# A list scheduler's model of the chip, rewritten: costs, PSUM hand-overs, TensorE bursts and the landing of first loads

## The chip, the core and the metric

The kernel runs on one core of a Trainium2 chip. Its engines take instructions from queues of their own, each strictly in order: TensorE (PE, matmuls, with its weight loads, PEld), ScalarE (ACT), VectorE (DVE), GpSimd (POOL) and SyncE (SP, which here only issues DMAs). Matmul results go to PSUM, which has eight banks; data otherwise lies in SBUF and comes from HBM by DMA. The metric is the device time of one execution in microseconds (us), lower is better. Runs of this kernel agree closely: 615.1 to 615.19 us.

## The reference, cut to what matters

Two layers over 256 tokens of width 1024, in float32. Each has a mixing sublayer with three groups of heads (neighbourhood "a", 4 heads; dilated "d", 6; grouped-query "c", 6 on 2 key/value heads) and a gated feed-forward network with a centred convolution of width 3 over the tokens.

```python
def mixer_sublayer(x, n1, w_in_l, qg, kg, rpb_l, og, w_out_l, tables):
    h = rms_norm(x, n1)
    proj = h @ w_in_l                       # 1024 x 2560
    qa, ka, va, qd, kd, vd, qc, kc, vc = jnp.split(proj, cuts, axis=-1)
...
    out_a = neighbourhood_attention(qa, ka, heads(va, H_NA), rpb_l, na_idx, na_dr, na_dc)
...
    out_d = dilated_window_attention(qd, kd, heads(vd, H_DIL), dil_idx, dil_val)
...
    out_c = gqa_block_attention(qc, kc, heads(vc, H_GKV))
    mix = jnp.concatenate([rms_norm(out_a, og[:NA_W]), rms_norm(out_d, og[NA_W:NA_W + DIL_W]),
                           rms_norm(out_c, og[NA_W + DIL_W:])], axis=-1)
    return x + mix @ w_out_l

def channel_sublayer(x, n2, w_gu, cw, cb, w_dn):
    h = rms_norm(x, n2)
    g, u = jnp.split(h @ w_gu, 2, axis=-1)  # 1024 x 5632
    g = depthwise_conv_centred(g, cw, cb)
    return x + (jax.nn.gelu(g, approximate=False) * u) @ w_dn   # 2816 x 1024

for l in range(DEPTH):
    x = mixer_sublayer(...)
    x = channel_sublayer(...)
```

## The kernel before

**Arithmetic.** Every matmul operand is split in two fp32r parts, hi and lo, and a product is made of three matmuls (`mm3`, L636: hi·hi, hi·lo, lo·hi). The weights stream from HBM in units of up to 128 x 2048 floats (`load`, tile `wp_raw`, four buffers); for each unit ACT copies the hi part (`wp_hi`) and DVE subtracts for the lo part (`wp_lo`), two buffers each (`split`, L607), in chunks of 384, 512 or 1024 columns. Activations are split in the same way: the transposed norm hT (`act_hT`), the transposed probabilities (tiles pTch and pTcl, in the trace `act_ch` and `act_cl`), the mixed heads mixT (`act_mixT_hi`, `act_mixT_lo`).

**Stages.** In each layer: the norm's transposes (pt_n1); the projections into PSUM tiles named after their group and half of the tokens (pj_dq, pj_dk, pj_dv, pj_cq, pj_ckv, pj_aqk, pj_av); per group the q and k norms and rotary positions (tiles z, then their transposes tr_q*, tr_k*); the heads in pairs; the output projections po0 to po2 added to the residual xs (in the trace `const_x`) with a group's factor (gs transposes, DVE sum, POOL rstd); then the second norm (pt_n2, h2) and eleven steps of gate G, up U and down D. One head is a chain through four engines: scores (PE), mask and maximum (DVE), two exponentials (ACT), reciprocal (DVE), scaling (ACT), four transposes tp (PE), hi copy pTch (ACT), lo copy pTcl (DVE), the weighted sum o of twelve matmuls for two heads (PE), mixT hi (ACT) and lo (DVE). The scores of two heads are one burst of twelve matmuls with 64-row operands, which use the two halves of the array side by side; the planner keeps them together (`together`). The matmuls of the projections and of po fill the time in which PE would wait for such a chain. Before the first real data PE runs 28 warming matmuls on a tile of ones: 13 with normal rank, 15 (WARM_MORE) with a rank 1000 later, to be used as fill. The neighbourhood bias is built through HBM: POOL repeats it, SP stores it (`scr`) and two loads read it back shifted (`nab`), and DVE masks it in three operations.

**Order.** Nothing above is issued directly: each call is recorded as an operation of class Plan (`add`, L253) with the engine, the operations before it, a rank (its place in the program plus an offset from `later`) and a cost in ns from `cost` (L416). `order` (L303) then simulates the engines. Over all engines' ready operations it takes again and again the one with the smallest (start time, rank); `at_of` (L318) gives the start as the latest of the operation's inputs, its engine's free time and the time at which a buffer or PSUM slot of its pool comes free; `at_of_burst` (L331) does so for a burst. The table HANDOVER (L215) adds the delay from one engine's end to another's start. A DMA is put down with its issue time, a wire shared by its ring and a latency. The result fixes the order of every engine's queue, SP's and POOL's DMAs too; `emit` (L408) issues it, so all instructions of the trace carry line L413. PSUM is two pools of four banks: psa (projections and outputs, `psa_a`) and psw (transposes, scores, o, G and U, `psw_w`). The order matters on the chip alone: which data an operation waits for is kept by semaphores whatever the planner believes.

## Time and profile before

| what | value |
|---|---|
| median of 3 runs | 615.19 us (615.1 to 615.19) |
| the profiled execution, its own time | 615.77 us |
| its span, first to last instruction | 614.0 us |
| mean granted TensorE clock | 0.999 |
| bytes over DMA | 121.44 MB, 198 GB/s |

The profile shows one execution. Its tables give the busy time of each engine, the same by stretches of time, the chain of work that ended last (followed back from the last instruction), and each instruction with its start, duration, engine and output<-input by tile names; `[0.42 <-ACT wp_hi L413]` at a row's end says that the engine was idle for 0.42 us before it and what ended that. Equal neighbours are put into one row with a count (x4), whose duration runs from the first start to the last end. PE's matmuls overlap, so the distance from start to start and not the duration is what one costs; idle time before a row is counted from the modelled end of the one before.

### The profile page before, as it was taken

Reading aid. Unit: us, or ns where it says so; the run is one execution under the profiler, and the core shown is the slowest. Engines: PE = TensorE matmul, PEld = TensorE weight load, DVE = VectorE, ACT = ScalarE, POOL = GpSimd, SP = SyncE. Lnnn points to the kernel's source line nnn. Section 1 sums busy time; section 2 is a strip of 40 time slices with the busy share of each in tenths; the row PEclk is TensorE's granted clock in tenths of the full one; section 3 lists DMA queues with packets and bytes.
Section 4 is the critical chain, followed back from the end, with each engine's and each line's share of the span. In section 5 each row is a group of like instructions: output and inputs, shape, how many; then the busy total and the mean of one; then the engine's idle time right before and its main releaser. Section 6 shows DMA issues by size and latency. Waiting matters only on the chain.

```text
span 614.0 us, 9882 instructions
## 1 busy us (share of the span) xinstructions
PE 604.2 (98%) x3484; PEld 525.1 (86%) x3484; DVE 488.2 (80%) x1000; ACT 428.2 (70%) x1064; POOL 83.4 (14%) x136
## 2 busy tenths in 40 slices
PE   8999999999999999999999999999999999999997
PEld 6998878888888888888899988887888888888885
DVE  4898989898778988877767797867977777787774
ACT  6788989686657676666588898866765556566561
POOL 2732231216000000000023212432000000000000
PEclk9999999999999999999999999999999999999999
DMA  8894212654698999988444744553655556556501
GB/s 281 269 288 161 95 44 79 226 188 164 209 239 293 330 335 320 310 276 284 153 151 155 242 137 173 197 183 112 231 202 176 175 202 191 171 187 206 188 18 68
DMA packets 85073, 121.44 MB, mean 198 GB/s; under 512 B 9864, under 2 KB 69608, under 8 KB 85024
## 3 DMA queue, kind: packets, MB, share of 16 engines
q1 hardware_dynamic: 82752, 112.17, 55.8%
q0 software_dynamic: 1728, 8.39, 4.0%
q8 instruction: 27, 0.44, 0.3%
q10 hardware_dynamic: 544, 0.26, 0.1%
q14 instruction: 22, 0.18, 0.1%
HBM read 110.93 MB, written 9.88 MB: 197 GB/s over the span
## 4 chain that ended last, share of the span: by engine, by line
PE 93%; ACT 2%; DVE 2%; issue 1%; DMA 1%; SPq 1%; POOL 0%; DVEq 0%; ACTq 0%
PE psw_w L413 50%; PE psa_a L413 43%; DVE const_x L413 1%; ACT act_s2k L413 1%; DMA const_x<-in_x_dram 1%; SPq L413 1%; ACT act_hT L413 1%; DVE act_hT L413 0%; ACT wp_hi L413 0%; DVE wp_lo L413 0%; POOL small_rstd L413 0%; ACT act_mixT_hi L413 0%; POOL small_ms L413 0%; DVE act_mixT_lo L413 0%; DVE small_ss L413 0%
## 5 line engine op out<-in xcount | busy, mean ns | idle before, releaser
L413 DVE TENSOR_TENSOR wp_lo<-wp_raw,wp_hi 128x512 fp32r<-128x512 f32 (+2 forms) x332 | 232.5, 733 | 58.4 <-ACT wp_hi L413 33.7
L413 ACT CAST wp_hi<-wp_raw 128x512 fp32r<-128x512 f32 (+2 forms) x332 | 202.3, 662 | 18.9 <-PE psw_w L413 9.6
L413 PE MATMUL psw_w<-act_hT,wp_hi 128*128 128x512 f32 x704 | 180.6, 394 | 0.4 <-DVE act_hT L413 0.4
L413 PEld LDWEIGHTS psw_w<-act_hT,wp_hi 128*128 128x128 f32 x704 | 127.9, 189 | 25.5 <-DVE act_hT L413 1.2
L413 PE MATMUL psa_a<-wp_hi,act_hT 128*128 128x384 f32 (+2 forms) x448 | 112.8, 333 | 1.4 <-ACT act_hT L413 1.3
L413 PEld LDWEIGHTS psw_w<-act_hT,wp_lo 128*128 128x128 f32 x704 | 97.7, 190 | 6.9
L413 PE MATMUL psw_w<-act_hT,wp_lo 128*128 128x256 f32 x704 | 102.5, 283 | 0.0
L413 PEld LDWEIGHTS psa_a<-wp_hi,act_hT 128*128 128x128 f32 x448 | 77.9, 189 | 4.6 <-ACT act_hT L413 1.8
L413 ACT COPY act_s2k<-psw_w 128x256 f32<-128x256 f32 x88 | 32.3, 371 | 63.8 <-PE psw_w L413 63.3
L413 PE MATMUL psa_a<-wp_lo,act_hT 128*128 128x384 f32 (+2 forms) x224 | 74.8, 334 | 0.0
L413 PE MATMUL psa_a<-wp_hi,act_ch 128*128 128x512 f32 x176 | 69.5, 395 | 0.0
L413 PE MATMUL psa_a<-wp_lo,act_ch 128*128 128x512 f32 x176 | 69.4, 395 | 0.0
L413 PE MATMUL psa_a<-wp_hi,act_cl 128*128 128x512 f32 x176 | 68.2, 395 | 0.0
L413 DVE TENSOR_TENSOR act_s2k<-psw_w,act_s2k 128x256 f32<-128x256 f32 x88 | 36.8, 421 | 12.9 <-ACT act_s2k L413 12.6
L413 PEld LDWEIGHTS psa_a<-wp_lo,act_hT 128*128 128x128 f32 x224 | 42.3, 189 | 1.9 <-DVE wp_lo L413 1.0
L413 PEld LDWEIGHTS psa_a<-wp_hi,act_cl 128*128 128x128 f32 x176 | 33.2, 188 | 7.7
L413 PEld LDWEIGHTS psa_a<-wp_hi,act_ch 128*128 128x128 f32 x176 | 33.2, 189 | 6.8
L413 PEld LDWEIGHTS psa_a<-wp_lo,act_ch 128*128 128x128 f32 x176 | 33.2, 189 | 6.8
L413 DVE SCALAR_TENSOR_TENSOR act_s2k<-act_s2k,act_cw,act_s2k 128x255 f32<-128x255 f32 x88 | 37.0, 480 | 1.4 <-ACT act_s2k L413 1.3
L413 ACT ACTIVATE act_s2k<-act_s2k,act_cw 128x256 f32<-128x256 f32 x44 | 24.1, 595 | 17.3 <-DVE act_s2k L413 17.0
L413 ACT ACTIVATE act_s2k<-act_s2k 128x512 f32<-128x512 f32 x22 | 13.9, 631 | 27.9 <-DVE act_s2k L413 27.9
L413 POOL TENSOR_TENSOR small_rstd<-small_ms,const_mh 128x6 f32<-128x6 f32 (+2 forms) x26 | 31.4, 1206 | 2.2
(112 smaller groups left out, 796.0 us busy)
## 6 DMA issues: line engine op xcount, KB each, us to landing
wp_raw<-in_w_gate_up_dram SPq DMA_DIRECT2D x44, 1024.0 KB, 5.2
wp_raw<-in_w_down_dram SPq DMA_DIRECT2D x22, 1024.0 KB, 4.9
wp_raw<-in_w_in_dram SPq DMA_DIRECT2D x14, 768.0 KB, 5.0
wp_raw<-in_w_in_dram SPq DMA_DIRECT2D x8, 1024.0 KB, 5.2
wp_raw<-in_w_out_dram SPq DMA_DIRECT2D x8, 768.0 KB, 4.9
dram_khi<-act_mixT_hi SPq DMA_DIRECT2D x4, 768.0 KB, 4.7
dram_klo<-act_mixT_lo SPq DMA_DIRECT2D x4, 768.0 KB, 5.7
wp_lo<-dram_klo POOLq DMA_DIRECT2D x4, 768.0 KB, 4.8
```

What stands on the lines that cost most here:

```text
L413: getattr(o.engine.real, o.method)(*map(real, o.args), **{k: real(v) for k, v in o.kw.items()})
```

## The change

Only the planner changes. The diff, cut to its core:

```diff
 ]
+LANDS = (4300, 3900, 5250, 3500, 6500, 7080, 7800, 8330, 8900, 9700, 10400, 10500, 10600)
+
+
 WARM, WARM_MORE, WARM_W = 13, 15, 256
 SUM_ACT, SCALE_ACT = ("dq", "dk", "cq"), ("dk",)
...
 HANDOVER = {
-    ("PE", "DVE"): 196, ("PE", "ACT"): 197, ("PE", "POOL"): 224, ("ACT", "DVE"): 131, ("ACT", "POOL"): 61,
-    ("ACT", "PE"): 240, ("DVE", "ACT"): 160, ("DVE", "PE"): 215, ("DVE", "DVE"): 127, ("DVE", "POOL"): 155, ("POOL", "DVE"): 60,
-    ("POOL", "ACT"): 60, ("POOL", "PE"): 150,
+    ("PE", "DVE"): 39, ("PE", "ACT"): 37, ("ACT", "DVE"): 33, ("DVE", "ACT"): 35, ("POOL", "DVE"): 34, ("POOL", "ACT"): 34,
+    ("DVE", "POOL"): 95, ("ACT", "POOL"): 90, ("POOL", "POOL"): 20, ("DVE", "DVE"): 34, ("ACT", "ACT"): 34,
 }
+
+
+def handover(a, b):
+    return HANDOVER.get((a, b), 52 if b == "PE" else 60)
 class Plan:
...
         ins = [v for v in views if not any(v is w for w in outs)]
         if method == "matmul" and not kw["start"]:
             ins.append(args[0])
-        o.ns, o.size = cost(engine.name, method, args, kw, ins)
+        o.ns, o.lat, o.size, o.kind = cost(engine.name, method, args, kw, ins)
         o.before, o.after, o.first, o.tiles = set(), [], [], []
         for v in ins + outs:
             t = v.tile
...
             for t in o.first:
                 t.turn = turns.get(t.pool, 0)
                 turns[t.pool] = t.turn + 1
-                t.left = t.users
-        free = dict.fromkeys(("PE", "ACT", "DVE", "POOL", "SP"), 550.0)
+                t.left, t.last = t.users, {}
+        free = dict.fromkeys(("ACT", "DVE", "POOL", "SP"), 550.0)
+        pe = None
         wires = {}
-        ready = {e: [] for e in free}
+        ready = {e: [] for e in ("PE", *free)}
         for i, o in enumerate(ops):
             o.at = 0.0
             if not o.left:
                 ready[o.engine.name].append(i)
+
+        def idle_at(e):
+            if e != "PE":
+                return free[e]
+            return 550.0 if pe is None else pe[0] + 3
+
+        def taken_at(since, e):
+            return since + (52 if e == "PE" else 36) if since > 0 else 0.0
+
         def at_of(o):
-            at = max(o.at, free[o.engine.name])
+            e = o.engine.name
+            at = max(o.at, idle_at(e))
             for t in o.tiles:
                 s = t.pool
                 if t.slot is not None:
                     at = max(at, t.since)
+                    if s.psum:
+                        for f, end in t.last.items():
+                            if f != e:
+                                at = max(at, end + handover(f, e))
                     continue
                 if t.turn != s.given or not s.free:
                     return None
-                at = max(at, min(s.free)[0])
+                at = max(at, taken_at(min(s.free)[0], e))
             return at
         def at_of_burst(burst):
-            at, wanted = 0.0, {}
+            at, wanted = idle_at("PE"), {}
             members = set(self.bursts[burst])
             for i in self.bursts[burst]:
                 o = ops[i]
                 if any(j not in members and not gone[j] for j in o.before):
                     return None
-                at = max(at, o.at, free[o.engine.name])
+                at = max(at, o.at)
                 for t in o.tiles:
                     if t.slot is not None:
                         at = max(at, t.since)
...
             for s, tiles in wanted.items():
                 if {t.turn for t in tiles} != set(range(s.given, s.given + len(tiles))) or len(s.free) < len(tiles):
                     return None
-                at = max(at, sorted(s.free)[len(tiles) - 1][0])
+                at = max(at, taken_at(sorted(s.free)[len(tiles) - 1][0], "PE"))
             return at
+
+        def run_on_pe(o, at):
+
+            half = o.kind == "half"
+            if pe is None:
+                return at + 109, o.ns, half, False
+            start, ns, was, open_ = pe
+            if half and was:
+                ld = max(start + 3, at)
+                if open_:
+                    return max(start + 4, ld + (0 if at <= start + 3 else 109)), o.ns, half, False
+                return max(start + 113, ld + 109), o.ns, half, True
+            if half or was:
+                return max(start + ns + 92, at) + 108, o.ns, half, True
+            return max(start + ns, max(start + 3, at) + (106 if o.kind == "turn" else 110)), o.ns, half, False
         done = []
         gone = [False] * len(ops)
...
                     s.given += 1
                     place = min(s.free)
                     s.free.remove(place)
-                    t.since, t.slot = place
-            free[e] = end = at + o.ns
+                    t.since, t.slot = taken_at(place[0], ""), place[1]
+            if e == "PE":
+                pe = run_on_pe(o, at)
+                end = pe[0] + o.ns + (218 if o.kind == "turn" else 163)
+            else:
+                free[e], end = at + o.ns, at + o.lat
             if o.method == "dma_start":
                 ring = e if i < self.first_loads else "SP"
-                end = max(end + 900, wires.get(ring, 0.0))
+                end = max(at + 1360, wires.get(ring, 0.0))
                 shared = 0.0
                 if i < self.first_loads:
                     shared = o.size if ring == "ACT" else min(o.size, 120 * max(0.0, wires.get("ACT", 0.0) - end))
                 wires[ring] = end + shared / 120 + (o.size - shared) / (280 if i < self.first_loads else 360)
                 end = wires[ring] + 900
+                if i < self.first_loads:
+                    end = LANDS[sum(p.method == "dma_start" for p in ops[:i])]
             for t in o.tiles:
                 t.left -= 1
                 t.until = max(t.until, end)
+                t.last[e] = end
                 if not t.left:
-                    t.pool.free.append((t.until + 170, t.slot))
+                    t.pool.free.append((t.until, t.slot))
             for j in o.after:
                 a = ops[j]
-                a.at = max(a.at, end + (170 if o.method == "dma_start" else HANDOVER.get((e, a.engine.name), 0)))
+                f = a.engine.name
+                if e != "PE" or f != "PE":
+                    a.at = max(a.at, end + (100 if o.method == "dma_start" else handover(e, f)))
                 a.left -= 1
                 if not a.left:
-                    ready[a.engine.name].append(j)
+                    ready[f].append(j)
         return done
     def emit(self):
...
     if method == "dma_start":
         w = out if isinstance(out, View) else args[1]
         small = min(out.shape[-1], args[1].shape[-1]) < 128
-        return 460, 4 * math.prod(w.shape) * (2 if small else 1)
+        spread = isinstance(args[1], bass.AP) and args[1].ap[0][0] == 0
+        size = 4 * math.prod(w.shape) * (2 if small else 2 if spread else 1)
+        return 620 if engine == "POOL" else 480, 0, size, None
     n = out.width()
     psum = any(v.tile.pool.psum for v in ins)
     if engine == "PE":
         if method == "transpose":
-            return 110, 0
+            return n / 2.25 + 2.5, 0, 0, "turn"
         n = args[2].width()
-        if args[1].dtype == F32:
-            return 108, 0
-        if args[1].shape[0] < P:
-            return n / 4.8 + 15, 0
-        return n / (2.4 if args[1].dtype == F32R else 1.2) + 2.5, 0
+        ns = {512: 231.6, 384: 174.5, 256: 118.0}.get(n, n / 2.25 + 2.5)
+        return ns, 0, 0, "half" if args[1].shape[0] < P else "full"
     if engine == "ACT":
-        extra = 93 * sum(isinstance(kw.get(k), View) for k in ("scale", "bias")) + 90 * ("accum_out" in kw)
-        return 0.833 * n + (47 if psum else 94) + extra, 0
+        extra = 88 * sum(isinstance(kw.get(k), View) for k in ("scale", "bias")) + 92 * ("accum_out" in kw)
+        ns = 0.833 * n + (53 if psum else 95) + extra
+        return ns, ns + (15 if "accum_out" in kw else 105), 0, None
     if engine == "DVE":
         if method in ("reduce_sum", "reduce_max"):
             n = args[1].width()
-        per = 1.04
-        if method in ("tensor_copy", "tensor_scalar_mul") and not psum:
-            per = 0.52
-        if method == "tensor_tensor_reduce":
-            per = 1.3
-        return per * n + (130 if method == "scalar_tensor_tensor" or method == "tensor_scalar_mul" and n > 16 else 70), 0
+        ns = 1.04 * n + (126 if method == "scalar_tensor_tensor" else 68)
+        return ns, ns + 82, 0, None
     if method == "memset":
-        return 40 + 0.9 * n, 0
-    if method == "tensor_copy":
-        return 3.4 * n, 0
-    if kw.get("op") == ALU.pow:
-        return 300 + 165 * n, 0
-    return 2.2 * n + 160, 0
+        ns = 190 + 0.83 * n
+    elif method == "tensor_copy":
+        ns = 0.92 * n + 100
+    elif kw.get("op") == ALU.pow:
+        ns = 560 + 150 * n
+    elif method == "tensor_scalar":
+        ns = 350 + 3.8 * n
+    else:
+        ns = 830 if out.width() == S else 350 + 3.1 * n
+    return ns, ns - 95, 0, None
 @with_exitstack
```

In words. The table HANDOVER becomes small (20 to 95 ns instead of 60 to 240), because `cost` now gives two figures for ACT, DVE and POOL: `ns`, how long the engine is occupied, and `lat`, when the result is there. PE has a model of its own (`run_on_pe`): a matmul starts after its weight load, half-row matmuls (kind "half") run two at a time, and switching between half and full costs extra; operations of PE that depend on PE's own no longer wait in the plan. A tile in PSUM remembers when each engine last used it (`t.last`), and an operation of another engine is put behind that: one engine at a time uses a bank. The DMAs' latency is 1360 ns from issue, POOL's issues cost 620 ns, and the end of each of the 13 first loads comes from the table LANDS. POOL's costs are new too, for example 830 ns for an addition over 256 columns where it was 723.

The programs of both hold the same instructions (3484 matmuls and transposes, the same DMAs); their order on each engine differs.

3 lines of the change are left out of this document (2 added, 1 removed).

## The prediction

> **What bounds the kernel now.** I read the page first: the busy shares, then the chain that ended last.
>
> ```profile
> span 614.0 us, 9882 instructions
> ...
> PE 604.2 (98%) x3484; PEld 525.1 (86%) x3484; DVE 488.2 (80%) x1000; ACT 428.2 (70%) x1064; POOL 83.4 (14%) x136
> ...
> PE 93%; ACT 2%; DVE 2%; issue 1%; DMA 1%; SPq 1%; POOL 0%; DVEq 0%; ACTq 0%
> ```
>
> TensorE (PE) is busy 98% of the span and makes 93% of the chain. The change neither adds nor removes a matmul (3484 in both builds, the DMAs are the same too), so what it can win is PE's idle time and no more. The second view, the busy time by stretches, shows where that is.
>
> ```profile
> core 0: us, PE busy (x) PEld busy (x) DVE busy (x) ACT busy (x) POOL busy (x), PEclk, DMA share, GB/s
> 0.00:14.46 14.46, 12.06 (x70) 9.39 (x70) 5.75 (x15) 8.94 (x23) 3.01 (x12) 1.00 0.86 275
> ...
> 60.00:80.00 20.00, 20.00 (x150) 17.82 (x149) 17.62 (x55) 18.99 (x56) 3.14 (x6) 1.00 0.29 96
> ...
> 82.00:86.00 4.00, 2.51 (x18) 1.94 (x17) 3.37 (x9) 3.08 (x10) 2.62 (x3) 1.00 0.00 0
> 86.00:100.00 14.00, 14.00 (x98) 11.70 (x97) 13.65 (x39) 12.68 (x41) 1.97 (x4) 1.00 0.11 39
> ...
> 120.50:128.00 7.50, 7.02 (x41) 5.58 (x42) 7.36 (x15) 7.19 (x20) 1.72 (x3) 1.00 0.35 136
> 128.00:309.00 181.00, 181.00 (x952) 155.06 (x953) 151.60 (x256) 118.81 (x219) 11.10 (x19) 1.00 0.80 265
> ...
> 382.00:385.00 3.00, 2.44 (x20) 2.24 (x20) 2.85 (x10) 3.00 (x12) 2.81 (x3) 1.00 0.00 0
> ...
> 420.00:426.00 6.00, 5.50 (x31) 4.57 (x32) 4.96 (x11) 5.83 (x15) 0.00 (x0) 1.00 0.02 4
> ```
>
> In the 181 us of the first feed-forward network PE never stops; the second has the same matmuls in the same order. Idle time that an order can touch lies in the attention half of layer 0 (1.49 us between 82 and 86), at the step from attention to the network (0.48 and 0.50), in layer 1's attention (0.56) and at the start (2.40). Of the rest, 60 to 80 says something else: PE at 20.00 of 20, ScalarE (ACT) at 18.99 and VectorE (DVE) at 17.62. What is reordered there has little room on three engines at once.
>
> **The start.** The planner now believes in 109 to 118 ns for a warming matmul and puts all 28 first; before, 15 went first, and the others filled gaps.
>
> ```profile
> 0.98 3.38 PE L413 MATMUL psw_w<-const_warm 128*128 128x256 bf16 x15 [0.98 <-POOL const_warm L413]
> ...
> 4.95 0.60 PE L413 MATMUL psw_w<-const_warm 128*128 128x256 bf16 x4
> ...
> 6.56 0.51 ACT L413 CAST wp_hi<-wp_raw 128x384 fp32r<-128x384 f32 x1 [3.53 <-DMA wp_raw<-in_w_in_dram]
> ...
> 7.49 0.61 PE L413 MATMUL psa_a<-wp_hi,act_hT 128*128 128x384 f32 x2 [1.29 <-ACT act_hT L413]
> ...
> 13.88 2.60 ACT L413 CAST wp_hi<-wp_raw 128x384 fp32r<-128x384 f32 x6
> ...
> 14.46 0.30 PEld L413 LDWEIGHTS psa_a<-wp_hi,act_hT 128*128 128x128 f32 x2 [0.42 <-ACT wp_hi L413]
> ```
>
> Fifteen cold ones took 3.38 us, or 0.21 each after the overlap of the last; warm ones start 0.11 apart (four in 0.60, the last of which fills 0.27 by itself). With the fast state from about 4.9 on, eighteen at 0.21 and ten at 0.11 end near 5.9. Five transposes follow at about 0.11 to 0.2, so the first hT0 on ACT starts near 6.6 and not at 6.97, but ahead of the two hi0 copies, which began at 6.56. The first real matmul therefore comes near 8.0, half a us later than 7.49. That does not move the end: from 6.56 to 16.5 ACT goes almost without a pause, and the matmuls of 14.46 wait for its hi1 copies at 13.88. ACT has the same 16 pieces before hi1 in both orders. I take +0.1, between −0.1 (ACT no longer waits for hT0 in between) and +0.5 (all of the later first matmul).
>
> The granted clock reads 1.00 over this whole stretch, the slow matmuls included, so here only the spacing tells the state: 0.21 up to 4.3, 0.11 from 4.95. The Trainium skill, TensorE: Matmul & The Clock Gate, section What's actually happening, says that the gate opens after about 3.4 us of activity in a free-running window, so that warming buys time and not a count, and that it closes again after an idle window of that length. The trace agrees with the opening; by the rest, the new idle time of about 1.3 us ahead of 8.0, like the 1.29 ahead of 7.49, closes nothing, and the sum stays.
>
> **Attention of layer 0.** The place that loses most is the second pair of the six GQA heads.
>
> ```profile
> 51.17 0.28 PE L413 MATMUL psa_a<-wp_lo,act_hT 128*128 128x256 f32 x1
> ...
> 51.53 0.28 PE L413 MATMUL psa_a<-wp_lo,act_hT 128*128 128x256 f32 x1
> ...
> 80.73 0.98 PE L413 MATMUL psw_w<-act_kc,act_qc 64*128 64x256 f32 x12
> ...
> 82.18 0.47 ACT L413 ACTIVATE const_v<-psa_a,small_rx 128x256 fp32r<-128x256 f32 x1 [0.22 <-PE psa_a L413]
> ...
> 83.00 0.47 ACT L413 ACTIVATE act_s2k<-psw_w,small_nm 128x256 f32<-128x256 f32 x1
> ...
> 83.71 0.36 PE L413 MATMUL psw_w<-act_ch,const_v 128*128 128x256 f32 x1 [1.13 <-ACT act_s2k L413]
> ...
> 85.06 0.46 DVE L413 SCALAR_TENSOR_TENSOR act_mixT_lo<-psw_w,const_gains,act_mixT_hi 128x256 fp32r<-128x256 f32 x1
> ...
> 85.58 0.44 PE L413 MATMUL psw_w<-const_ident,act_z 128*128 128x128 f32 x2 [0.36 <-DVE act_mixT_lo L413]
> ...
> 383.63 0.66 PE L413 MATMUL psw_w<-const_ident,act_s2k 128*128 128x128 f32 x4 [0.56 <-ACT act_s2k L413]
> ...
> 384.05 0.37 PE L413 MATMUL psw_w<-act_ch,const_v 128*128 128x256 f32 x1
> ```
>
> The score burst s_c02/s_c03 ends at 81.7; its bank comes free when ACT's second exponential of head c02 ends at 83.47, and the weighted sum o_06, which takes that bank over, starts at 83.71. So 2.0 us pass from burst to bank. Behind the burst, before has two projection matmuls and four transposes. Three 256-column matmuls take 0.36 (51.17 to 51.53), one 0.12; with transposes at 0.11 (four in 0.42, from 383.63 to 384.05) that is 0.7 us of cover, and 1.3 us of stall. The new order has twenty such matmuls and four transposes there: 2.4 + 0.44 = 2.8 us, more than 2.0. The stall goes: −1.3. It can hold because before spent that fill early: two projection matmuls pj_av were left at the burst, after has 38 left, and the burst stands 36 matmuls earlier on PE. The transposes at 85.58 (waiting for a bank whose last reader is the DVE's 85.06) come behind those twenty too: −0.36.
>
> What is late next? The chain of the heads (scores, maximum, exponential, transposes, hi and lo copies, weighted sum) is asked for up to 36 × 0.12 = 4.3 us earlier against the projections. To serve it, ACT's copies hi11 and hi12 and the V evictions, and DVE's lo10 and lo11, are moved behind it; they feed projections that come later as well, so most of the shift is paid in work that nobody waits for. Two transposes of z_cq01 are an exception: they move ahead of the burst s_d02.
>
> ```profile
> 54.58 0.55 DVE L413 TENSOR_TENSOR act_z<-act_z,act_sw 128x384 f32<-128x384 f32 x1
> ...
> 56.24 0.27 PE L413 MATMUL psw_w<-const_ident,act_z 128*128 128x128 f32 x1
> ```
>
> z is done at 55.13; the new place of the two transposes is five 512-column matmuls earlier, near 55.1. DVE puts z ahead of one lo copy (pTcl_d00) now, so it may come 0.6 earlier and cost nothing, or not, with a wait up to 0.6. I take +0.3. For this stretch −1.3 −0.36 +0.3 = −1.4; bounds −1.7 and 0 (all of it met again in a later wait).
>
> **The mask tables and SP's queue.** The store of the bias rows and the two loads nab0 that read it back go ahead of raw8 and raw9.
>
> ```profile
> L413 DVE SCALAR_TENSOR_TENSOR act_nab<-act_nab,const_na x6: 739/752/761, 44.2 to 203.0; 128x576 f32<-128x576 f32 x6
> ...
> 35.05 1.97 SPq L413 DMA_DIRECT2D act_nab<-dram_scr  x2
> ...
> 39.84 4.36 DVE L413 TENSOR_TENSOR wp_lo<-wp_raw,wp_hi 128x384 fp32r<-128x384 f32 x8
> ...
> 46.71 5.71 PE psa_a L413 x46
> ```
>
> The eight copies from 39.84 on are lo7 and lo8, so lo8 began near 41.7, and nab0 came behind it at 44.2. Now all three nab0 operations (0.75 each) stand in front of lo8. If their data lands no sooner than before, DVE is held 44.2 − 41.7 = 2.5 us and has 3 × 0.75 = 2.25 to do before lo8, whose first copy would end near 47.1 instead of 42.4; the matmuls on it begin with the run of 46.71 or shortly ahead of it, so PE would stand up to 1.0. But the loads now pass raw9 on SP's queue and raw8 comes behind the store, so the data should land sooner, by about the length of a load. I take 0, with 0 and +1.0 as bounds.
>
> **The step to the network, layer 0.**
>
> ```profile
> 119.84 0.40 PE L413 MATMUL psa_a<-wp_hi,act_mixT_lo 128*128 128x512 f32 x1
> ...
> 120.07 0.40 PE L413 MATMUL psa_a<-wp_hi,act_mixT_hi 128*128 128x512 f32 x1
> ...
> 120.59 0.44 PE L413 MATMUL psw_w<-const_ident,const_x 128*128 128x128 f32 x2
> ```
>
> A 512-column matmul takes 0.23 (119.84 to 120.07), so the transposes could have started at 120.30; they waited 0.29 for DVE's residual. The new order sends the norm's transposes gs20 out four matmuls (0.92) sooner, so the residual is ready sooner and the 0.29 goes. DVE and ACT put the copies lo18, lo19, hi18, hi19 behind the h20 chain, for which G0_00 now waits at 127.85: of the 0.48 idle between 120.5 and 128 (0.09 of it belongs to the wait before) I take 0.3. Together −0.6; bounds −0.8 and 0.
>
> **Layer 1** has the same pattern, and the 0.56 ahead of 383.63 is its form of the stall at 83.71.
>
> ```profile
> ...
> 420.12 0.88 PE L413 MATMUL psw_w<-const_ident,const_x 128*128 128x128 f32 x6 [0.48 <-DVE const_x L413]
> ...
> 424.03 0.69 DVE L413 TENSOR_TENSOR wp_lo<-wp_raw,wp_hi 128x512 fp32r<-128x512 f32 x1
> ...
> 425.43 0.88 PE L413 MATMUL psw_w<-const_ident,const_x 128*128 128x128 f32 x6 [0.37 <-DVE const_x L413]
> ```
>
> That stall is covered by the same shift of fill; the transposes of z_cq11 get 0.1 to 0.55 shorter cover, of which I take 0.3: −0.3, bounds −0.6 and +0.2. At the end of its attention the lo69 copy leaves its place (one of 0.69, at 424.03) ahead of the residual and goes into earlier idle time; the 0.37 at 425.43 goes, the 0.48 at 420.12 stays, since the same residual and the same PE order stand before it: −0.4, bounds −0.85 and 0. Stores on SP swap one place with raw loads there, and POOL's loads of stored weights go behind small operations; what they feed is a unit or more away from its use: 0. The feed-forward order is the same: 0.
>
> **Sum:** +0.1 −1.4 +0 −0.6 −0.3 −0.4 = −2.6, and I keep −2.5. The profiled execution took 615.77 us (its span of 614.0 and 1.8 around it), 0.6 over the median of the runs, 615.19; a difference of 2.5 from either gives 612.7 in the runs. Bounds of all terms: −0.1 −1.7 −0.8 −0.6 −0.85 = −4.05, and +0.5 +1.0 +0.2 = +1.7.
>
> **Rivals.**
>
> *The heads' chain is late (slower).* In 86 to 100 DVE has 13.65 of 14 and in 60 to 80 ACT has 18.99 of 20. If DVE can't pull the lo copies pTcl forward, because each meets one weight copy of 0.69 that is already in the queue, PE waits 0.69 once at each of the six pairs of d and c heads in layer 0: +4.1. Against the −2.5 that is +1.6: 616.8. It makes the whole thing slower than the measurable bound from 0.62 a pair on, (2.5 + 1.23)/6. For it: no slack on three engines. Against it: DVE as a whole does no more work, the deferred copies are those, and only one wait of the six was there before.
>
> *The stalls move (same).* What 83.71, 85.58 and 383.63 win is met again in the next waits, since ACT and DVE and not PE then set the pace of the heads; left are the steps to the network, −0.6 −0.4, with +0.1 at the start and +0.3 for z: 614.6. For it: the same rows.
>
> *DVE waits for the masks.* All of the −2.5, with the +1.0 for nab0 and another +0.5 from what DVE then does late: 614.2, within the bound below too.
>
> *The planner is wrong and the change doesn't do what it says.* It counts 118 ns for a cold matmul that took 0.21, and places first loads by a table; all its later times are then off by half a us, and waits between DMA, ACT and PE fall otherwise than planned: no gain, and +0.5 at the start, 615.7.
>
> **How the numbers follow.** I call a difference under 0.2% (1.23 us) the same, which is what a measurement of this kernel can't tell from none. The forecast, 612.7, gets 0.56, its own range being 611.1 to 613.9; the late chain 0.20; moved stalls, masks and a planner gone wrong together 0.24. Some 0.02 of the forecast's chance ends above 613.96: faster 0.54, same 0.26, slower 0.20. The range goes from 610.9, the lower bound with 0.2 for what I haven't seen, to 616.6, about the middle of the late chain.
>
> **What would show it.** Right: PE busy without a pause from 80 to 86, the row of o_06 without an ACT releaser; transposes of const_x without a DVE releaser at 120 and 425; the first pj matmul near 8.0 but hi1's matmuls at 14.4 to 14.6; feed-forward stretches at 181 of 181. Wrong: new waits of 0.3 us or more of PE for pTcl, mixT_lo or act_z between 55 and 100; DVE idle ahead of act_nab on a DMA; matmuls at twice their spacing after 8 us; or a hi1 that comes after 14.9.

## The result, and the profile after

The changed kernel is slower: 620.64 us (617.0 to 623.99, 9 runs) against 615.19 us (614.78 to 615.69, 9 runs) of the kernel before on the same chip, a ratio of 1.0077 (of the means, as all ratios here) with an interval of 1.005 to 1.0105. Its nine runs lie further apart than those of before, and the time goes with the mean granted clock: 617.0 and 617.02 us at 1.000, 618.52 at 0.999, and 619.6 to 623.99 in the six at 0.994 to 0.998. The profiled execution is the one of 623.99, so the 8.2 us between the two spans overstate the 5.45 between the medians.

The page of the changed kernel (span; busy times; shares of the chain that ended last):

```profile
span 622.2 us, 9882 instructions
...
PE 609.7 (98%) x3484; PEld 527.8 (85%) x3484; DVE 484.6 (78%) x1000; ACT 428.3 (69%) x1064; POOL 85.1 (14%) x136
...
PE 87%; DMA 4%; DVE 4%; ACT 2%; issue 1%; POOL 1%; SPq 1%; DVEq 0%; ACTq 0%; POOLq 0%
```

The work is the same. The chain shows what is new: DMA is now 4% of it, where before it was 1%, and PE lost 6 points. PE's busy time grew by 5.5 us for the same 3484 matmuls; the slow clock below is a part of that. Where the span grew, by the start times of the same matmuls in the two traces (from one named matmul to the next):

| stretch | after − before, us |
|---|---|
| start to the first matmul on hi1 | +3.51 |
| to the first down matmul of layer 0 (attention, step, G0_00) | −1.64 |
| to the first projection of layer 1 (the feed-forward network) | +1.90 |
| to the first down matmul of layer 1 | +4.45 |
| the rest | 0.00 |

**Start.** The timeline of the changed kernel, first 18 us:

```profile
0.98 6.02 PE L459 MATMUL psw_w<-const_warm 128*128 128x256 bf16 x28 [0.98 <-POOL const_warm L459]
...
7.46 1.28 ACT L459 ACT_TABLE_LOAD   x1 [7.46 <-DVE const_gains L459]
8.76 0.84 ACT L459 ACTIVATE act_hT<-psw_w,const_gains 128x256 fp32r<-128x256 f32 x2
...
10.05 0.94 PE L459 MATMUL psa_a<-wp_hi,act_hT 128*128 128x384 f32 x2 [2.30 <-ACT wp_hi L459]
...
17.97 0.62 PE L459 MATMUL psa_a<-wp_hi,act_hT 128*128 128x384 f32 x2 [0.38 <-ACT wp_hi L459]
```

Three things are to be seen. The 28 warming matmuls take 6.02 us, 0.21 each to the last. The table load of ACT stands right in front of its first activation, hT0, and waits with it for DVE's `const_gains`, which is read from the first transpose; in before, the same load had this row:

```profile
1.74 1.28 ACT L413 ACT_TABLE_LOAD   x1 [1.74 <-issue]
```

ACT's first piece there was a hi0 copy, which waited for its DMA until 6.56; the load ran ahead of that wait. And PE then has 2.30 us without work. How the clock goes on in this profile is in the view by stretches (length, busy time and count of PE, PEld, DVE, ACT and POOL, then PEclk, DMA share, GB/s):

```profile
8.00:9.00 1.00, 0.00 (x0) 0.00 (x0) 0.00 (x0) 0.99 (x2) 0.00 (x0) 1.00 1.11 314
...
10.00:11.00 1.00, 0.95 (x4) 0.85 (x5) 1.00 (x4) 1.00 (x4) 0.00 (x0) 0.58 1.03 376
...
12.00:13.00 1.00, 1.00 (x5) 1.00 (x4) 0.64 (x3) 1.00 (x3) 0.00 (x0) 0.50 1.02 344
...
13.50:14.00 0.50, 0.50 (x4) 0.50 (x4) 0.23 (x1) 0.24 (x1) 0.00 (x0) 0.93 1.04 372
...
416.00:418.00 2.00, 0.41 (x2) 0.00 (x0) 1.14 (x2) 0.27 (x1) 1.25 (x2) 1.00 0.86 233
...
419.00:420.00 1.00, 1.00 (x5) 0.83 (x4) 0.00 (x0) 0.00 (x0) 0.00 (x0) 0.88 0.85 238
420.00:421.00 1.00, 1.00 (x4) 0.71 (x4) 0.00 (x0) 0.00 (x0) 0.00 (x0) 0.50 0.60 217
...
423.00:424.00 1.00, 1.00 (x5) 0.76 (x5) 0.00 (x0) 0.00 (x0) 0.39 (x1) 0.92 0.00 0
```

Behind the idle gap of 2.30 us the clock is at one half from about 10.2 to 13.6, behind one of 1.82 us ahead of 418.24 from about 419.8 to 423.2. (The edges come from the means: 0.58 in a stretch of 1.00 is 0.84 us at one half, so it fell at 10.16.) PE counts as fully busy there; it is only slower. A gap of this length did not always have this behind it, as p_new_start below shows.

**Feed-forward network, layer 0.** The timeline of the changed kernel at a stored weight, and the same place before:

```profile
214.44 0.37 SPq L459 DMA_DIRECT2D wp_raw<-in_w_out_dram  x1
...
226.34 1.66 ACT L459 CAST act_mixT_hi<-wp_raw 128x512 fp32r<-128x512 f32 x3 [2.62 <-DMA wp_raw<-in_w_out_dram]
...
227.91 0.36 ACT L459 COPY act_s2k<-psw_w 128x256 f32<-128x256 f32 x1
...
228.17 0.62 ACT L459 CAST act_ch<-act_s2k 128x512 fp32r<-128x512 f32 x1
...
228.84 0.50 PE L459 MATMUL psa_a<-wp_hi,act_ch 128*128 128x512 f32 x1 [0.90 <-ACT act_ch L459]
```

```profile
223.58 0.62 ACT L413 CAST act_mixT_hi<-wp_raw 128x512 fp32r<-128x512 f32 x1
...
224.10 0.62 ACT L413 CAST act_ch<-act_s2k 128x512 fp32r<-128x512 f32 x1
...
224.62 0.62 ACT L413 CAST act_mixT_hi<-wp_raw 128x512 fp32r<-128x512 f32 x1
```

While the first network runs, the output weights of layer 1 are split once for later: loaded, copied to hi by ACT and to lo by DVE (in the trace through buffers named `act_mixT_hi` and `act_mixT_lo`), stored by SP, and read back by POOL's loads in layer 1. I call them stored weights. Before, `act_ch`, for which the down matmuls wait, stood between their copies; after, all three stand ahead of it, and wait for a load that took 11.88 us. Counted from start to start of the matmuls, PE loses 1.06 us there and 0.57 at the next lo part.

**Layer 1.** POOL and PE of the changed kernel, then POOL of before:

```profile
409.42 0.57 POOL L459 DMA_DIRECT2D wp_lo<-dram_klo  x1 [2.18 <-PE psa_a L459]
...
410.35 0.71 POOL L459 TENSOR_TENSOR small_rstd<-small_ms,const_mh 128x2 f32<-128x2 f32 x1
...
411.02 0.60 POOL L459 DMA_DIRECT2D wp_hi<-dram_khi  x1
...
418.24 0.50 PE L459 MATMUL psa_a<-wp_hi,act_mixT_hi 128*128 128x512 f32 x1 [1.82 <-DMA wp_hi<-dram_khi]
```

```profile
401.63 0.57 POOL L413 DMA_DIRECT2D wp_lo<-dram_klo  x1 [4.15 <-PE psa_a L413]
402.20 0.54 POOL L413 DMA_DIRECT2D wp_hi<-dram_khi  x1
```

The hi load of the stored weight hi66 goes out 1.60 us after that of lo66 instead of 0.57, behind the small operations `small_ms` and `small_rstd`, and lands at 418.19, when PE has been waiting for it. PE loses 1.98 us from start to start, and the slow clock follows.

### The profile page after: what moved, and what is told of

It is laid out like the page before. It is cut to its first block, busy times and chain, and to the rows that moved or that the text cites. A ratio compares the mean times of both kernels' runs of the same rounds, so it can differ in the third digit from the quotient of the medians.

```text
span 622.2 us, 9882 instructions
## 1 busy us (share of the span) xinstructions
PE 609.7 (98%) x3484; PEld 527.8 (85%) x3484; DVE 484.6 (78%) x1000; ACT 428.3 (69%) x1064; POOL 85.1 (14%) x136
## 4 chain that ended last, share of the span: by engine, by line
PE 87%; DMA 4%; DVE 4%; ACT 2%; issue 1%; POOL 1%; SPq 1%; DVEq 0%; ACTq 0%; POOLq 0%
PE psw_w L459 47%; PE psa_a L459 40%; DMA wp_raw<-in_w_out_dram 2%; DMA wp_hi<-dram_khi 1%; ACT act_s2k L459 1%; DVE wp_lo L459 1%; DVE const_x L459 1%; DMA const_x<-in_x_dram 1%; POOL small_rstd L459 1%; DVE act_hT L459 1%; SPq L459 1%; ACT wp_hi L459 0%; ACT act_hT L459 0%; POOL small_ms L459 0%; DVE act_mixT_lo L459 0%
## 5 line engine op out<-in xcount | busy, mean ns | idle before, releaser
L459 ACT CAST wp_hi<-wp_raw 128x512 fp32r<-128x512 f32 (+2 forms) x332 | 202.1, 662 | 14.4 <-PE psw_w L459 8.9
L459 PE MATMUL psa_a<-wp_hi,act_hT 128*128 128x384 f32 (+2 forms) x448 | 115.3, 337 | 2.7 <-ACT wp_hi L459 2.7
L459 PE MATMUL psa_a<-wp_hi,act_cl 128*128 128x512 f32 x176 | 69.7, 396 | 0.4 <-DVE act_cl L459 0.4
```

The source lines that it names most:

```text
L459: getattr(o.engine.real, o.method)(*map(real, o.args), **{k: real(v) for k, v in o.kw.items()})
```

## The experiments

Most kernels here splice orders: both planners (`order_was`, `order_new`) run over the same operations, `first(seq, name)` is the place of a tile's first PE instruction in a sequence, `joined` takes each part's operations that are not yet taken, and the result is issued; the diffs are shortened to the line that sets the order. All have 3484 matmuls as before, but splicing makes seams of its own. Every one was timed against the kernel before on its chip. Untouched starts of different executions differ by up to 1.1 us in the traces, so single profiles are used for places and medians for sizes. A stall's size is counted from start to start, less what the matmul itself costs, and its time is the start of the last matmul ahead of it.

### Which stretch

New start, rest as before:

```diff
+    seq = joined(new[: first(new, "pj_dq00", "hi1")], was)
```

> The reverse: the changed kernel's start, everything behind it in exactly the order of before. Theory A: 615.2 plus 3.0 to 3.5, so 618.2 to 618.7, with a spread over the runs of some 2 us, because the clock closes in some of them. If the start is hidden later: 615.2 to 616.

617.95 us against 615.08, ratio 1.0047 (1.0032 to 1.0061): the start alone costs 2.9 by the medians. The rest of its trace is before's. But no run took 617.95: three took 616.8 to 617.03 us at a granted clock of 1.000, which is 1.7 to 2.0 above before, and three 618.87 to 619.6 at 0.997 to 0.993, 3.8 to 4.5 above. The profile is of a run of the first kind, 617.03 us:

```profile
9.21 0.62 PE L621 MATMUL psa_a<-wp_hi,act_hT 128*128 128x384 f32 x2 [2.29 <-ACT wp_hi L621]
...
10.00:11.00 1.00, 1.00 (x8) 0.84 (x6) 0.97 (x3) 1.00 (x5) 0.00 (x0) 1.00 1.00 347
```

Its idle gap is as long as the changed kernel's 2.30, and the clock stays at 1.00.

Start as before, rest new:

```diff
+    seq = joined(was[: first(was, "pj_dq00", "hi1")], new)
```

> The start as before (every engine's order up to the first matmul on hi1), everything behind it in exactly the changed kernel's order. Theory A (the start costs 3.0 to 3.5 us): 617 to 617.6, with stalls left near 227 and 416. Theory that the start's loss is hidden later, because ScalarE and VectorE set the pace: 620 or more. If 612.7 came out, the start would be the whole of the loss.

615.47 us, ratio 1.0015 (1.0002 to 1.0027), against 615.08, a time that none of the three cases expected. Without the start the remainder nearly balances: gains in layer 0 and a stall of 1.81 us near 410.

Attention of layer 0 alone, up to the first gate matmul (`G0_00`), and then up to the first down matmul (`pd000`), so that the step to the network is whole:

```diff
+    seq = joined(was[: first(was, "pj_dq00", "hi1")], new[: first(new, "G0_00")], was)   # p_mixer0
+    seq = joined(was[: first(was, "pj_dq00", "hi1")], new[: first(new, "pd000")], was)   # layer0_new
```

> The start as before, the attention of layer 0 and its step to the network in the changed order, everything from the first gate matmul of layer 0 in the order of before. If the stalls of 83.7, 85.6, 120.6 and 127.9 are gone without others in their place, as the changed kernel's trace suggests: 612.6 to 613.3. If they are met again in the network behind it, or the chain of the heads is late: 615 or more.

615.07 us against 615.08, ratio 1.0 (0.9992 to 1.0009). The stall at 83 is gone here too, but the seam makes two new ones, 0.92 at 122.57 and 0.83 at 126.14, in the step to the network. It is not a measure of the attention.

> The start as before, everything of layer 0 from there to the first down matmul in the changed order (the step to the network and its G0 included, which the run with the cut at the first gate matmul cut in two), the rest as before. If the two stalls that appeared in that run at 122.6 and 126.1 (0.92 and 0.83 us) came only from the cut: they are 0.25 or less, and the time is 615.1 - 1.9 (80 to 100) - 0.6 (115 to 128) + 0.7 (30 to 60) + 0.1, so 613.2 to 613.6. If the changed step to the network costs them itself: 615.

**613.34 us** against 615.23, ratio 0.997 (0.9959 to 0.9981). In its view by stretches

```profile
80.00:86.00 6.00, 6.00 (x50) 5.80 (x49) 6.00 (x16) 6.00 (x20) 2.16 (x3) 1.00 0.24 87
86.00:100.00 14.00, 14.00 (x92) 11.38 (x91) 11.45 (x31) 11.97 (x37) 1.64 (x3) 1.00 0.12 39
116.00:128.00 12.00, 11.88 (x65) 9.45 (x64) 10.77 (x21) 10.14 (x26) 3.42 (x5) 1.00 0.45 150
128.00:307.00 179.00, 179.00 (x941) 153.27 (x940) 149.65 (x252) 116.80 (x214) 10.79 (x18) 1.00 0.81 266
```

PE has no pause from 80 to 100. Layer 0's order is worth 1.9 us by itself.

Only layer 1 new, and only the first network new:

```diff
+    seq = joined(was[: first(was, "pj_dq10")], new)                                       # layer1_new
+    seq = joined(was[: first(was, "pd000")], new[: first(new, "pj_dq10")], was)           # ffn0_new
```

> As before up to the first projection matmul of layer 1, from there in the changed order. Theory: the changed order of layer 1 loses where the stored weights of the last output projections land late (1.8 us near 410) and where the exponential's table load stands in front of the heads (0.67 near 351), and wins 0.3 to 0.7 elsewhere: 616.3 to 617.2. If the late landing near 410 is only a consequence of the changed layer 0: 615.

616.46 us against 615.23, ratio 1.0023 (1.0013 to 1.0032): +1.2, with a stall of 1.50 us at 410.31 and one of 0.67 at 350.85.

> Only the first feed-forward network in the changed order: SP's raw loads and stores of weights swap places there, ScalarE takes the copies of the kept weights three in a row. Theory: the loads then land after ScalarE wants them in some executions (11.9 us from issue to landing at 214 in the changed kernel's profile) and TensorE stands 0.5 to 3 us: median 615.6 to 616.6, runs spread over 1.5 us or more. If those stalls came from the later clock of the start: 615.1, runs within 0.9 us as before.

619.24 us (616.6 to 620.96), ratio 1.0062 (1.0044 to 1.0079): the stretch that the prediction called unchanged costs 4.0, far more than was expected here too, some 0.6 of it at the seam to layer 1. In its trace PE stalls five times between 225 and 279, by 0.27 to 1.43 us.

### The start

The changed kernel with one more instruction, a small ACT copy of a constant tile that is there from the beginning, so that the table load has something early to stand in front of:

```diff
 nc.gpsimd.memset(minus_half, -0.5)
+early = const.tile([P, 32], F32, tag="early", name="early")
+nc.scalar.copy(early, minus_half)
```

> The changed kernel with one instruction more: ScalarE copies a 128x32 tile right after POOL's first memsets, so that the activation table is loaded near 1.7 us and not behind the wait for the gains (7.46 to 8.74 in the changed kernel's profile). Theory A, the table load lies on the path at the start and the 2.3 us of idle TensorE that it makes let the clock close: first projection matmul near 8.7 instead of 10.05, no stretch at clock 0.50 between 10 and 13.5, time 617 to 618.5. Rival B, the slow warming matmuls alone make the loss: first matmul earlier, but the time stays at 620 or more. Rival C, the loss is in the loads of the later stages: 619 to 620.6.

618.21 us (616.39 to 620.75) against 615.08, ratio 1.0049 (1.0031 to 1.0067); the changed kernel had 1.0077. The load now runs at 1.22, the first hT0 at 7.25, and PE's idle time ahead of the first projection is 1.33 us, after which the clock stays at 1.00:

```profile
1.22 1.28 ACT L459 ACT_TABLE_LOAD   x1 [1.22 <-PEq L1489]
...
8.54 0.62 PE L459 MATMUL psa_a<-wp_hi,act_hT 128*128 128x384 f32 x2 [1.33 <-ACT wp_hi L459]
```

All six runs had a granted clock of 0.999 or 1.000, where the changed kernel had three of nine. The start of this profile is 2.9 us shorter than the changed kernel's; this profile was taken of its slowest run, which lost 3.9 in the first network.

The same copy in p_new_start:

> The changed kernel's start, everything behind it as before, with one ScalarE copy of a 128x32 tile in front that brings the table load to about 1.3 us. Theory: of the 2.7 to 2.9 us that the changed start costs, the table load is 1.28 and what the clock loses in some runs comes from the idle time that it makes; the rest, 1.0 to 1.1, is the 28 warming matmuls: 616.2 to 616.5, no run above 617. If the clock closes without the table load too: median above 617, with runs of 618.5 and more.

616.32 us against 615.15, ratio 1.0022 (1.0013 to 1.003). By the medians the place of the table load makes 1.6 of the start's 2.9 us (617.95 − 616.32; the befores differ by 0.07). That is two things. Among runs at a clock of 0.998 or more it makes 0.6 (616.84, the median of three, against 616.25, of ten). The rest comes of the clock: three of six runs of p_new_start were below that, and one of the eleven here, 618.57 us at 0.997. Some 1.2 are left for the 28 warming matmuls ahead of the transposes and the order behind them; no run separates these two.

### The stored weights in layer 1

p_old_start, with POOL's hi load put right behind the lo load of the same stored weight:

```diff
+for u in (66, 67):
+    seq.remove(hi[u])
+    seq.insert(seq.index(lo[u]) + 1, hi[u])
```

> The start as before, the rest changed, but the POOL load of hi66 directly behind that of lo66 (before: behind two small operations of the group factor), and hi67 directly behind lo67 (before: behind an addition). If POOL's queue makes the load late: hi66 issued 1.0 us sooner, the stall near 410 shrinks from 1.8 to 0.8, time 0.5 to 1.0 under that of the kernel with the start as before (615.5). If the later release of the buffer by TensorE sets it: the stall stays at 1.5 or more and the time at 615.5.

616.17 us (613.46 to 620.44), ratio 1.0022 (1.0002 to 1.0042). The stall near 410 falls from 1.81 to 0.15 us: hi66 is issued 0.57 behind lo66 again.

```profile
407.48 0.57 POOL L631 DMA_DIRECT2D wp_lo<-dram_klo  x1 [2.19 <-PE psa_a L631]
408.05 0.54 POOL L631 DMA_DIRECT2D wp_hi<-dram_khi  x1
408.66 0.19 POOL L631 TENSOR_SCALAR small_ms<-small_ss 128x2 f32<-128x2 f32 x1
```

The median doesn't show the gain: this kernel's runs spread over 7 us, and in its profile the first network loses 3.4 us, which the edit doesn't touch. The place is settled by this run, its size is read from "best" below.

### The first network: which queue

First with SP's queue exchanged against the engines'. The two give the buffers out in other orders than either parent:

```diff
+    return merged(seq, sp=was)      # ffn0_sp_was: engines new, SP as before
+    return merged(was, sp=seq)      # ffn0_sp_new: SP new, engines as before
```

> Only the first feed-forward network in the changed order, as in the run that lost 4 us there, but with SP's queue of loads and stores in the order of before. Theory E (the engines' order: ScalarE's two copies of a kept weight, which wait for its DMA, stand in front of the conv and gelu copies): the stalls of ScalarE on the kept raw loads stay, 617 to 619.5. Theory Q (SP's queue: loads and stores in changed places make the loads late): 615.2 to 615.8.

> The reverse: SP's queue in the first feed-forward network in the changed order, everything else exactly as before. Theory E: 615.2 to 615.8, because a late load blocks nothing. Theory Q: 617 to 619.5.

619.45 us (ratio 1.0065, 1.0053 to 1.0077) and 617.5 (1.004, 1.0028 to 1.0052), against 615.15. Both are slower than before, and the second differs in stretches that its edit doesn't touch (+0.69 us in the second network): the other buffers confound it. So each engine's queue was then exchanged alone, with buffers given out as before:

```diff
+    seq = joined(was[: first(was, "pd000")], new[: first(new, "pj_dq10")], was)
+    lanes = {e: [i for i in (seq if e in CHANGED else was) if ops[i].engine.name == e] for e in ENGINES}
```

> Only SP's queue in the first feed-forward network in the changed order (stores of kept weights and small loads change places with raw loads by one), every engine's order and every buffer as before. Theory E (engines): 615.2 to 615.8. Theory Q (SP's queue): 616.5 to 617.9, as in the run before, whose buffers had moved too.

615.25 us against 615.35, ratio 1.0007 (0.9997 to 1.0018). SP's new order alone costs nothing that can be measured (one of its twelve runs took 619.11 us, at a granted clock of 0.997).

> TensorE, ScalarE and VectorE in the changed order in the first network, SP's queue as before, buffers given in order of time (the earlier run of this kind had them given otherwise). Theory E: 618 to 619.5, ScalarE waiting on raw loads of kept weights ahead of the gelu copies. Theory Q: under 616.

PE, ACT and DVE new: 617.53, ratio 1.0036 (1.0024 to 1.0048), a little under theory E's range and far from theory Q's.

> As the run before, but TensorE's order as before (its 55 moved matmuls are down matmuls that were split in twos). If ScalarE's and VectorE's orders alone make the loss: the same time as with all three engines, 618 to 619.5. If TensorE's order has a part in it: 0.5 or more lower.

ACT and DVE new: 617.73, 1.0037 (1.0025 to 1.0049). PE's order has no part in it that can be measured.

> Only VectorE's order changed in the first network, ScalarE's as before. If ScalarE's kept copies ahead of the conv copies are the cause: 615.2 to 615.9. If VectorE's order (next weight's lo copy ahead of the conv, the mask operations pulled forward) makes it: 617 or more.

DVE alone new: 618.34, 1.0058 (1.0046 to 1.007). The expectation, which had ACT's copies as the cause, fell: DVE's order alone makes +3.0. Its trace shows two PE stalls that before has not, 1.68 us at 275.45 and 1.06 at 312.10. ACT's order alone was not run.

Two last kernels move one thing each on DVE, all else as before (on another chip than lane_dve):

```diff
+    at = dve.index(klo68[0]) - 5                         # pair_early: the two lo operations of a stored weight
+    dve = [i for i in dve if i not in klo68]
+    dve[at:at] = klo68
...
+    dve[at : at + 7] = dve[at + 4 : at + 7] + lo51      # x_early: three residuals ahead of four lo copies
```

> The order of before in everything but two instructions: VectorE's two lo operations of the stored weight klo68 stand five and seven places further ahead, where the changed kernel's planner has them, which is in front of two lo copies of 1024 columns, the product of gate and up and one lo part of that product. Theory: they wait there for ScalarE's khi68 copies (3.83 us of VectorE's idle time in lane_dve), and what stands behind them makes the down matmuls late by the 1.68 us that lane_dve shows at 275.45; so 615.2 + 1.7 = 616.9, with one TensorE stall of 1.5 to 1.8 near 275 and none else that before has not. Rival: the mask operations moved ahead near 210 hold the buffers and are the cause; then 615.2 here, no new stall.

617.78 us against 615.38, ratio 1.0043 (1.0029 to 1.0056): 2.4, where 1.7 was expected. The timeline of this kernel, then of before:

```profile
272.02 1.29 DVE L647 TENSOR_TENSOR act_mixT_lo<-wp_raw,act_mixT_hi 128x512 fp32r<-128x512 f32 x2 [3.83 <-ACT act_mixT_hi L647]
...
273.23 1.22 DVE L647 TENSOR_TENSOR wp_lo<-wp_raw,wp_hi 128x1024 fp32r<-128x1024 f32 x1
...
274.70 1.22 DVE L647 TENSOR_TENSOR wp_lo<-wp_raw,wp_hi 128x1024 fp32r<-128x1024 f32 x1
275.83 0.68 DVE L647 TENSOR_TENSOR act_s2k<-act_s2k,act_s2k 128x512 f32<-128x512 f32 x1
...
276.55 0.62 ACT L647 CAST act_ch<-act_s2k 128x512 fp32r<-128x512 f32 x1 [3.24 <-DVE act_s2k L647]
...
277.22 0.51 PE L647 MATMUL psa_a<-wp_hi,act_ch 128*128 128x512 f32 x1 [1.53 <-ACT act_ch L647]
```

```profile
273.29 0.69 DVE L413 TENSOR_TENSOR act_s2k<-act_s2k,act_s2k 128x512 f32<-128x512 f32 x1
...
274.00 0.62 ACT L413 CAST act_ch<-act_s2k 128x512 fp32r<-128x512 f32 x1
...
276.17 0.39 PE L413 MATMUL psa_a<-wp_hi,act_ch 128*128 128x512 f32 x1
```

DVE reaches the two operations, waits 3.83 us for ACT's copies of the same stored weight, and two lo copies of 1.22 and the product of gate and up come out behind them, the product at 275.83. Before had it at 273.29, in a trace that runs 0.6 us later up to here, so it is 3.2 us late. The down matmul pays 1.69 us. The rival, the mask operations moved ahead near 210, is not needed: the stalls elsewhere stay as before.

> The order of before in everything but one place on VectorE at the end of the first feed-forward network: three of the four residual updates stand ahead of the four lo copies of the next layer's first weight instead of behind them. Theory: the fourth update then has the four copies ahead of it (1.95 us in lane_dve) and the norm's transposes wait for it, 1.06 us in lane_dve; 615.2 + 1.1 = 616.3, with a stall of about 1 us near 312. Rival: that wait comes of lane_dve's late transfers and not of the place; then 615.2.

616.48 us against 615.38, ratio 1.0018 (1.0009 to 1.0027), with the stall of 1.06 us at 309.82. The two moves make 2.4 + 1.1 = 3.5, and lane_dve 3.0: they account for its +3.0 to within 0.5. This second stall is not one of the changed kernel, though: the four copies stand ahead of the last residual there too (it starts at 314.81), but PE's own order has three projection matmuls, from 315.09, in front of the transposes that wait for it (315.72), and the trace has no stall above 0.3 us between 300 and 330.

### A version that beats both

Layer 0 new up to the first down matmul, the first network as before, layer 1 new with the hi loads behind their lo loads:

```diff
+    seq = joined(was[: first(was, "pj_dq00", "hi1")], new[: first(new, "pd000")], was[: first(was, "pj_dq10")], new)
+    # and the hi loads of 66 and 67 as in kept_first
```

> Start as before; layer 0 up to the first down matmul in the changed order; the first network as before; layer 1 in the changed order, with the POOL loads hi66 and hi67 directly behind lo66 and lo67. From the parts: 613.3 (layer 0) + 1.2 (layer 1 changed) - 1.4 (its stall at 410 shrinks from 1.5 to 0.15) = 613.1, range 612.7 to 613.6. If layer 1's loss isn't in that stall: 614 or more.

613.66 us against 615.15, ratio 0.9977 (0.9968 to 0.9985): faster than before, just above the expected range, and no better than layer0_new. The stall near 410 is gone and the 0.67 at 349.48 stays, so layer 1's new order, once mended, wins nothing (+0.07 us over its stretch in the profile). By the medians against the befores it adds 0.4 to layer0_new's −1.9 where layer1_new added 1.2: some 0.8 us is the price of the hi loads' place.

## Why the prediction was wrong, point by point

**Start, forecast +0.1 (−0.1 to +0.5): wrong, +2.9.** The step that failed is "That does not move the end: from 6.56 to 16.5 ACT goes almost without a pause". It counted ACT's 16 pieces, which is right, and left out the table load in front of the first of them. Before, the load ran at 1.74, ahead of a hi0 copy; with hT0 as ACT's first piece it runs at 7.46, behind the wait for `const_gains`, and hT0 at 8.76. By new_start_early this place is worth 1.6 us in the medians, 0.6 of it without a loss of clock. "With the fast state from about 4.9 on" failed as well: in the changed kernel's profile all 28 stay at 0.21 and end at 7.0, not 5.9 (in p_new_start's they end at 6.2). The first projection came at 10.05 and not near 8.0, hi1 at 17.97 and not at 14.4 to 14.6. The sentence on the gate took the Trainium skill's idle window of about 3.4 us (TensorE: Matmul & The Clock Gate, What's actually happening) and let 1.3 us pass. That part agrees with early_table, where 1.33 us closed nothing; but the gap became 2.30 us, and behind it the clock did close, well short of the window that the Trainium skill states. It need not: p_new_start's profile has a gap of 2.29 and kept 1.00. The start costs 1.7 to 2.0 us in the runs of p_new_start at a clock of 1.000 and 3.8 to 4.5 in the others; the 2.9 is the median between them. That these others lost their clock at the start is likely, since nothing else in them differs from before, but none of them was profiled. The slow clock was named as a sign of being wrong ("matmuls at twice their spacing after 8 us").

**Attention and step of layer 0, forecast −1.4 and −0.6: right.** layer0_new measured −1.9. The stalls of 83.71 and 85.58 are gone, and the row of 80 to 86 reads 6.00. The split of the −1.9 between the two terms was not measured: p_mixer0 was spoilt by its seam. The z_cq01 term, +0.3, was a stall of 0.16 us at 54.85 in the changed kernel. The masks, 0 with +1.0 as bound, cost nothing to be seen: layer0_new has them in their new place.

**Rivals.** "The heads' chain is late" would have given six waits of 0.69 in layer 0; there is none, so that it ended on the right side only by luck. "The stalls move" fell with layer0_new. "The planner is wrong" was nearest: its +0.5 at the start had the right sign, but the mechanisms were others.

**The feed-forward order, forecast "is the same: 0": wrong, and the costliest reading error.** I looked at PE's order, took it for the same, and looked at no other. It is nearly the same: in the first network 55 down matmuls are moved, and lane_act_dve shows that this costs nothing. The step that failed is to take this for the order of every engine. DVE and ACT are reordered there, and lane_dve, pair_early and ffn0_new put +2.4 to +4.0 on it. For pair_early the cause is shown: two operations on a stored weight, needed over a hundred us later, stand ahead of work that the next matmuls need, and hold up the queue by a wait for another engine. A stall at the same place, 1.26 to 1.44 us in front of a down matmul at 278 to 280, is in the profiles of early_table, ffn0_new and kept_first; in ffn0_new's, ACT's copies wait 3.11 us for their DMA there first. In the changed kernel's own profile it is another stored weight, at 226, with ACT's copies ahead of `act_ch`; that this is ACT's form of the same is read from its rows and wasn't isolated. How much it costs varies: the first network was +0.05 us in the profile of p_old_start, +1.9 in the changed kernel's, +3.9 in early_table's. Behind a load that may land early or late, a fixed order is a bet. What makes that load land late stays open: the median landing of the eight loads of its kind (768 KB) went from 4.9 to 8.6 us, and lane_sp shows that SP's order alone doesn't cost time.

**Layer 1, forecast −0.3 and −0.4: gains right, one cost missed.** The 0.56 of 383.63 is gone; the 0.48 at 420.12 stays (0.49 at 428.21), as forecast, and the 0.37 at 425.43 fell to 0.17 at 432.77. The step that failed is "POOL's loads of stored weights go behind small operations; what they feed is a unit or more away from its use: 0". In before hi66 is issued 8.3 us ahead of its use (402.20 to 410.52) and its load takes 6.2. In the changed kernel it is issued 5.2 us ahead of where PE would have used it (411.02 to 416.26), 1.0 of the loss by its place in the queue and the rest because PE has less work in between, and the load takes 7.2. That makes the 1.98 us of stall, 1.5 and 1.8 in layer1_new and p_old_start, and in the profiled run the half clock behind it costs some 1.6 us more (eight matmuls between 420 and 423, each 0.2 late). kept_first and best, with the place as before, have at most 0.15 us of it. A second new stall, 0.67 us at 356.47, stands behind a table load of 1.28 us for the exponentials at 352.89, with three weight copies interleaved; no run took it apart.

**Sum.** +2.9 at the start, −1.9 in layer 0, +1.2 in layer 1, together +2.2, and 2.4 to 4.0 in the first network with its seam: 4.6 to 6.2 against the 5.45 measured. That these medians meet it is partly luck, for the parts do not simply add: p_old_start has all of them but the start and lies 0.4 above before, where they give 1.7 to 3.3. The granted clock has a share that the parts do not show apart: the two runs of the changed kernel at 1.000 lie 1.8 above before, and the 0.994 of the median run is worth up to 0.006 × 620.6 = 3.7 us of PE's time (an estimate, and an upper bound, since PE does not set the pace everywhere). The forecast's −2.0 for layer 0 was the part I had studied most, and the three terms set to about 0 held the result.

## What to carry to other kernels

When a scheduler's costs change, compare the order on every engine's queue, in the stretches that look finished too: an order that looks equal on the bounding engine says nothing about who feeds it. A term is 0 only if its cover has been counted from issue to use with the landing times in the trace; work for later must stand behind work for now on an in-order queue, above all when it waits for a DMA. Ask what the first instruction of each engine is: a one-time cost such as a table load can end up behind its wait. Where runs fall into two groups, read the groups and not the median between them.

## What the runs showed of the hardware that was not expected

- In the changed kernel's profile the granted clock fell to 0.50 behind idle gaps of 2.30 and 1.82 us (by their rows), 0.1 and 1.5 us after work had begun again, and stayed there for 3.4 us both times. The length of the gap alone does not decide it: 2.29 us in p_new_start's profile left the clock at 1.00, as 1.64 us in p_old_start's and 1.33 in early_table's did. What decides it is not shown. The length of the slow stretch agrees with the window of some 3.4 us in the Trainium skill (TensorE: Matmul & The Clock Gate, What's actually happening); the gaps are shorter than the idle window stated there, and here the measurement decides.
- The same 28 warming matmuls took 6.02 us in the changed kernel's profile, at 0.21 us each to the last, 5.84 in new_start_early's, 5.48 in early_table's and 5.19 in p_new_start's: how many are slow is not a matter of their count. The granted clock read 1.00 all through these stretches.
- A table load can take the wait of the activation behind it: in the profiles of the changed kernel and of p_new_start it began with the release of `const_gains`, at 7.46 and 6.63. It need not: in before it ran at 1.74, while the copy behind it waited for its DMA until 6.56; the runs do not show what makes the difference. It took 1.28 us in each. The Trainium skill, ScalarE: Activation LUTs, section What ACT_TABLE_LOAD costs, has about 1283 ns for the load itself, with which the rows agree.
